# Decoder trunk on one core: the end by token halves, the sample's stores on ScalarE's queue, and the order of work at the borders

## The chip, the cores and the metric

One core of a Trainium2 chip runs the whole kernel. The metric is the device time of one execution in microseconds (us). The time before is the median of three runs; a further execution was profiled. The engines are PE (matmuls), DVE (VectorE), ACT (ScalarE), POOL (GpSimd) and SP (SyncE, which here issues the loads of weights and the stores).

## The reference

One decoder layer for 256 prompt tokens and 8 x 4 sample tokens, width 2048, all in fp32:

```
x = x + 1/2 * post1(SwiGLU_1(pre1(x)))
x = x + post2(HybridMixer(pre2(x)))
x = x + 1/2 * post3(SwiGLU_2(pre3(x)))
```

Each pre and post is an RMS norm over the 2048 columns with a gain. SwiGLU takes x to twice 5632 columns and back. The mixer projects x to q, k, v, a rank-16 product for the decay (a_lr), a gate r and the HGRN parts; it runs two gated linear recurrences (GLA and HGRN2) in chunks, norms, gates and projects back. The outputs are x of the prompt and of the sample tokens, and the final states.

## The kernel before

**Layout and matmuls.** Activations stay transposed: x[k], k = 0 to 15, is a tile of 128 columns of the model by T = 288 tokens (256 of the prompt, 32 of the samples). Weights come in units of 128 x 1024 fp32. ACT copies a unit to a high part wh (L96), and DVE subtracts it from the raw one to give the low part wl (L97), both in PE's fast fp32r format. Activations are split in the same way (xh, xl). A product is three matmuls: xh by wh, xl by wh, xh by wl (L591 to L593), with 288 tokens moving. The class Weights keeps up to four split units ahead of PE (HL_BUFS, three raw buffers); its field `behind` holds an instruction behind which the next split is ordered on DVE and ACT. A function block computes four 128-column outputs over all k, in PSUM tiles drawn from five banks, and evicts each.

**What sets the order.** A scheduler orders the instructions of each engine's queue, from the program's dependencies and its own estimates of time. `tc.issue_after(ins)` adds an order for what is traced inside it: behind ins on ins's engine, with no semaphore. Each engine serves its own queue strictly in order.

**Borders.** Ahead of a sub-layer, PreNorm (L473 to L505) sums the squares of x beside the first products: tick1(k) is called behind step k of a block, and at step `at` it calls rstd (L455 to L471). That issues the two `pre` matmuls (L460), then for FFNs a square root on ACT and a reciprocal (L463) on DVE of 128 x 288 to give the factor rt; in the mixer (`tmps` given) it goes by a logarithm, an exponential and two DVE steps (L470, L471). The products are not scaled until then, and their eviction multiplies by rt. Behind a sub-layer, post_norm (L558 to L575) sums the squares of its output y, spreads the factors over all partitions through PE (L445), and updates x: y by the factor (L562), x plus y by the gain (L563), then the split into xh on ACT (L257) and xl on DVE (L258). The first EARLY = 4 x tiles are covered by a stand-in: PE multiplies the old x and y (`fill`) with the first weights for one of the four outputs. UPDATED = 8 tiles are updated in this function.

**Mixer's start.** The first block (qk0) fills q and k of GLA's first heads; the second (v0) computes v, with a tick at each of its 16 steps k: at 11 the mean's matmuls, at 8 the scaling of the low-rank weights, at 12 a_lr, which multiplies x by the 16 columns (L1445, 16 products of 16 rows, 32 matmul instructions), adds four partial sums on DVE (L1449), scales them by rt (L1450) and splits them into high and low (L1451 to L1457). v's eviction multiplies by rt (L979). gla_decay multiplies them up later (zp, L1463). The next block that takes the banks is qk1.

**The end.** The last block of the last FFN writes y12 to y15. Its evictor ev (L750 to L775) adds a PSUM tile to y (L755), squares y (sq_add; for y15 on DVE at L422) and scales it by the gain to z (L764, ACT). by_token turns z to token-major with two PE transposes (L730) and an ACT copy (L731) into zT; samples does so for the 32 sample tokens (L737, L738) into zS. finish (L795 to L822) sums the squares per token with matmuls against ones (L432), takes root (ACT, L160) and reciprocal (DVE, L437) of two columns for the prompt's two halves of 128 tokens, then, behind POOL copies (L803), of one for the samples. Nine additions of 128 x 512 on DVE (L809) give the outputs: three pairs of the prompt, the samples, then the fourth pair. SP stores each prompt piece as it is ready (L822, 256 KB), and the samples in four stores (L815, 64 KB) between the third pair's and the fourth's.

Of the kernel before, what the change touches and what calls it, by code (L numbers as in the profile page):

```python
# [16 lines left out]
P = 128  # L17
# [109 lines left out]
def trunk_kernel(ctx, tc, x_prompt, x_sample, state_gla, state_hgrn, norm_gains, f1_in, f1_out, f2_in, f2_out,  # L127
# [37 lines left out]
    def mmtile(name):  # L165
        return mmp.tile([P, 512], F32, name=name, tag="mm")

    def auxtile(name):
        return aux.tile([P, 512], F32, name=name, tag="aux")
# [303 lines left out]
    class PreNorm:  # L473
# [12 lines left out]
        def tick1(self, k):  # L486
            if k < 8:
                with tc.issue_after(self.split[0]), tc.issue_after(self.split[1]):
                    for j in (2 * k, 2 * k + 1):
                        sq_add(x[j], j)  # L490
                    if k == 7:
                        self.parts = high_low(acc)
            if k == self.at:
                ins = rstd(rt, self.parts, self.name, self.tmps and self.tmps())

                behind = [G.memset(gate[:, 0:1], 0.0).ins, V.tensor_copy(gate[:, 1:2], epst).ins,
                          S.activation(gate[:, 2:3], epst, AF.Copy).ins]
                self.behind = behind
                with ExitStack() as es:
                    for i in behind:  # L500
                        order(i, ins)
                        es.enter_context(tc.issue_after(i))
                    for f in self.late:
                        f()
# [47 lines left out]
    def post_norm(gcol, gnext, lasts, name, fill):  # L552

        parts = [[sq[:, c:c + P] for c in (0, P, T - P)] for sq in (acc, *(sq for sq, _ in lasts))]
        rc, inss = mean_cols(auxtile(name), parts, 0, 3, True)
        fill.old_mean, fill.mean = inss[0], inss[-1]
        if name != "postm":
            with tc.issue_after(lasts[-1][1]):  # L558
                W.ahead(1)

        def update(k):
            V.tensor_tensor(y[k], y[k], fill.scale[:, 0:T], op=ALU.mult)  # L562
            ins = V.scalar_tensor_tensor(x[k], y[k], gcol(k), x[k], op0=ALU.mult, op1=ALU.add).ins  # L563
            return *split_x(gnext, k), ins

        def go():
            fill.scale, fill.row = spread(rc, name + "s")
            for k in range(UPDATED):
                with ExitStack() as es:
                    if k == 1:  # L570
                        es.enter_context(tc.issue_after(ins[2]))
                    ins = update(k)
                if k == AHEAD:
                    W.behind = ins[0]

        fill.go = go
        return update
# [64 lines left out]
    def ffn(tag, gcol, gnext, pn, before, fill=None):  # L642
# [3 lines left out]
        with ExitStack() as pools:  # L646
# [93 lines left out]
            def do_out(c, n):  # L740
                hs = [hid.pop(c + i) for i in range(n)]
                if final:
                    zt, xt = final_tiles[0:2]
                end = c + n == NCH
                if end:
                    act_set(AF.Sqrt)
                    if not final:
                        border[0].fill.old()
                for o in range(4):
                    def ev(f, ps):  # L750
                        k = 4 * o + f
                        if c == 0:
                            S.activation(y[k], ps, AF.Copy)
                        else:
                            V.tensor_tensor(y[k], ps, y[k], op=ALU.add)  # L755
                        if end:
                            sq = sq_add(y[k], k, 0, KT - 2, KT - 1)
                            if k >= KT - 1:
                                lasts.append(sq)
                            if not final:  # L760
                                border[0].fill.new(k)
                            else:
                                z = fp.tile([P, T], F32, name="z", tag="z", bufs=4)
                                S.activation(z, y[k], AF.Copy, scale=gcol(k))  # L764
                                if o < 3:
                                    turn32(z, f)
                                    if f == 3:
                                        move32(o, *zt, (G, nc.sync) if o == 2 else (G,))
                                else:
                                    if f > 1:  # L770
                                        by_token(zs[f - 2], k - 2, *zt)
                                    zs.append(z)
                    block(f"out{tag}_{c}_{o}", 4 * n, lambda k: [t[:, k % 4, :] for t in hs[k // 4]], ev,
                          tail=2 if end and o == 3 else 1, hold=end and o == 3)
                    k = 4 * (c - 4) + o  # L775
                    if final and 0 <= k < KT:
                        turn32(x[k], o)
                        if o == 3:
                            move32(c - 4, *xt, (G,))
# [3 lines left out]
            if final:  # L783
                zt, xt = final_tiles[0:2]

                def rest():
                    by_token(zs[2], KT - 2, *zt)
                    by_token(zs[3], KT - 1, *zt)
                    samples(zs, zt[1])

                finish(lasts[0][0], rest, zt, xt)
                return None
        return post_norm(gcol, gnext, lasts, f"post{tag}", border[0].fill), border[0]

    def finish(last, rest, zt, xt):  # L795

        (zT, zS), (xT, xS) = zt, xt
        ms = auxtile("postf")
        rc, _ = mean_cols(ms, [[sq[:, t * P:(t + 1) * P] for t in range(2)] for sq in (acc, last)], 0, 2, True)
        four = []  # L800
        for sq in (acc, last):
            r = sqp.tile([P, 4, TS], F32, name="sq4", tag="pn")
            G.tensor_copy(r, sq[:, TP:T].unsqueeze(1).broadcast_to([P, 4, TS]))  # L803
            four.append([r.rearrange("p a b -> p (a b)")])
        rest()
        rcs, _ = mean_cols(ms, four, 2, 3, False)

        def add(o, z, x, t):
            V.scalar_tensor_tensor(o, z, rc[:, t:t + 1] if t < 2 else rcs, x, op0=ALU.mult, op1=ALU.add)  # L809

        for s in range(4):
            if s == 3:
                add(zS, zS, xS, 2)
                for q in range(4):
                    nc.sync.dma_start(y_sample[:, :, q * 512:(q + 1) * 512].rearrange("b t c -> (b t) c"),  # L815
                                      zS[q * TS:(q + 1) * TS, :])

            o = (hlp if s else rawp).tile([P, 2, 512], F32, name=f"o{s}", tag="wh" if s else "raw")
            for t in range(2):
                k = slice(4 * s, 4 * s + 4)  # L820
                add(o[:, t].rearrange("p (k c) -> p k c", c=P), zT[:, k, t], xT[:, k, t], t)
                nc.sync.dma_start(y_prompt[0, t * P:(t + 1) * P, s * 512:(s + 1) * 512], o[:, t])  # L822


    def mixer(pn, border):
        with ExitStack() as mx:
# [614 lines left out]
            def a_lr():  # L1441
                ps = mmtile("a_lr")
                for k in range(KT):
                    q = k % 4 * TS
                    PE.matmul(ps[q:q + 16, 0:T], ag[:, k, :], x[k], start=k < 4, stop=k >= KT - 4)  # L1445
                G.memset(alr32[0:32, :], 0.0)
                S.activation(alr32[0:16, :], ps[0:16, 0:T], AF.Copy)
                for q in range(TS, P, TS):
                    V.tensor_tensor(alr32[0:16, :], alr32[0:16, :], ps[q:q + 16, 0:T], op=ALU.add)  # L1449
                V.tensor_tensor(alr32[0:16, :], alr32[0:16, :], rt[0:16, :], op=ALU.mult)  # L1450
                S.activation(alr[0:32, :], alr32[0:32, :], AF.Copy)  # L1451
                V.tensor_tensor(alr[32:64, :], alr32[0:32, :], alr[0:32, :].bitcast(F32), op=ALU.subtract)
                S.activation(alr[64:96, :], alr32[0:32, :], AF.Copy)
                for g in range(2):
                    c = slice(256 * g, 256 * g + 256)
                    S.activation(aw[:, c], aw32[g][0:96, 0:256], AF.Copy)
                    V.tensor_tensor(aw[64:96, c], aw32[g][64:96, 0:256], aw[64:96, c].bitcast(F32), op=ALU.subtract)  # L1457
# [30 lines left out]
            for g in range(2):  # L1488
# [5 lines left out]
                if g == 0:  # L1494
                    vt = vtiles("g0")
                    block("v0", KT, xrhs, ev_v(*vt, 2, 1), 
                          tick=lambda k: (pn.tick1(k), scale_lr() if k == 8 else a_lr() if k == 12 else None))
                    with tc.issue_after(W.recent[0]), tc.issue_after(W.recent[1]):
                        lower_bounds()

# [143 lines left out]
```

## Time and profile before

| | us |
|---|---|
| median of three runs (2248.39 to 2248.95) | 2248.5 |
| the profiled execution | 2247.12 |
| its span | 2245.3 |
| PE busy in the span | 2233.0 (99%) |
| DVE busy | 1386.3 (62%) |
| ACT busy | 1022.8 (46%) |
| POOL busy | 171.2 (8%) |

The mean granted clock of TensorE was 0.998. The DMA engines moved 171 GB/s in the mean. In a timeline a line gives the start, the length, the engine (SPq and ACTq: DMAs that SP or ACT issues), the line of the kernel, the operation, the tile written <- the tiles read, their shapes, and how many alike were merged; in brackets stands how long the engine had been idle and whom it waited for. The length of merged rows runs from the first one's start to the last one's end.

### The profile page before, as it was taken

To read this page: it belongs to the slowest core of one execution; us is meant where nothing else is said; L and a number is where in the kernel's file an instruction comes from. 1 tells how busy PE (TensorE), PEld (TensorE's weight loads), DVE (VectorE), ACT (ScalarE), POOL (GpSimd) and SP (SyncE) were. 2 spreads that over 40 slices of the span, in tenths; PEclk is the share of its full clock that TensorE was granted. 3 is DMA by queue.
4 is the path that set the end of the run, shared out by engine and by line. 5 is a ranking of instruction groups with operands and counts; after the bars stand their busy time and mean duration, and the time that the engine had idled before them with its cause. 6 is when DMAs were issued, how large, how long until landed. Compare 5 with 4: busy or idle time off the path is not lost.

```text
span 2245.3 us, 43325 instructions
## 1 busy us (share of the span) xinstructions
PE 2233.0 (99%) x17832; PEld 2218.3 (99%) x17832; DVE 1386.3 (62%) x2252; ACT 1022.8 (46%) x1556; POOL 171.2 (8%) x311
## 2 busy tenths in 40 slices
PE   9999999999999999999999999999999999999998
PEld 9999999999999999999999999999999999999998
DVE  7545545554555568888888755944555465545646
ACT  6443333333334345555676654544333333333344
POOL 2000000000000001333000000530000000000005
PEclk9999999999999999999999999999999999999999
DMA  7555555555555554667565554665555555555555
GB/s 223 171 169 162 167 168 162 168 167 163 169 165 182 170 164 141 194 197 213 174 172 169 178 184 130 195 186 164 165 169 164 165 169 164 165 169 163 166 166 152
DMA packets 226758, 384.28 MB, mean 171 GB/s; under 512 B 21106, under 2 KB 60544, under 8 KB 226560
## 3 DMA queue, kind: packets, MB, share of 16 engines
q1 hardware_dynamic: 213968, 365.15, 51.8%
q0 software_dynamic: 10416, 16.18, 2.7%
q8 instruction: 140, 2.29, 0.4%
q10 hardware_dynamic: 2176, 0.18, 0.1%
q14 instruction: 58, 0.48, 0.1%
HBM read 363.75 MB, written 11.80 MB: 167 GB/s over the span
## 4 chain that ended last, share of the span: by engine, by line
PE 99%; DVE 0%; POOL 0%; ACT 0%; issue 0%; DVEq 0%; POOLq 0%
PE gate L591 10%; PE gate L593 10%; PE gate L592 10%; PE out L592 8%; PE up L593 8%; PE up L591 8%; PE up L592 8%; PE out L593 8%; PE out L591 8%; PE hfq L591 2%; PE hfq L593 2%; PE hfq L592 2%; PE mo L593 2%; PE mo L591 2%; PE mo L592 2%; PE hi L591 1%
## 5 line engine op out<-in xcount | busy, mean ns | idle before, releaser
L97 DVE TENSOR_TENSOR wl<-raw,wh 128x1024 fp32r<-128x1024 f32 (+1 forms) x676 | 821.8, 1217 | 616.7 <-ACT wh L96 612.8
L96 ACT ACTIVATE wh<-raw 128x1024 fp32r<-128x1024 f32 (+1 forms) x676 | 711.5, 1054 | 1018.8 <-PE gate L592 308.8
L591 PE MATMUL gate<-xh,wh 128*128 128x288 f32 x1660 | 489.4, 296 | 0.0
L593 PE MATMUL gate<-xh,wl 128*128 128x288 f32 x1660 | 487.7, 295 | 0.0
L592 PE MATMUL gate<-xl,wh 128*128 128x288 f32 x1660 | 485.7, 295 | 0.0
L592 PE MATMUL out<-hl,wh 128*128 128x288 f32 x1408 | 416.1, 296 | 0.0
L593 PE MATMUL up<-xh,wl 128*128 128x288 f32 x1408 | 415.6, 295 | 0.0
L593 PE MATMUL out<-hh,wl 128*128 128x288 f32 x1408 | 415.3, 295 | 0.0
L592 PE MATMUL up<-xl,wh 128*128 128x288 f32 x1408 | 415.1, 295 | 0.0
L591 PE MATMUL up<-xh,wh 128*128 128x288 f32 x1408 | 415.0, 295 | 0.0
L591 PE MATMUL out<-hh,wh 128*128 128x288 f32 x1408 | 414.1, 294 | 0.0
L591 PEld LDWEIGHTS gate<-xh,wh 128*128 128x128 f32 x1660 | 311.3, 188 | 0.9 <-DVE z L1533 0.2
L593 PEld LDWEIGHTS gate<-xh,wl 128*128 128x128 f32 x1660 | 311.4, 188 | 0.2 <-DVE wl L97 0.2
L592 PEld LDWEIGHTS gate<-xl,wh 128*128 128x128 f32 x1660 | 310.7, 188 | 0.3
L593 PEld LDWEIGHTS out<-hh,wl 128*128 128x128 f32 x1408 | 265.0, 188 | 0.0
L591 PEld LDWEIGHTS out<-hh,wh 128*128 128x128 f32 x1408 | 264.9, 188 | 0.0
L592 PEld LDWEIGHTS out<-hl,wh 128*128 128x128 f32 x1408 | 264.7, 188 | 0.0
L593 PEld LDWEIGHTS up<-xh,wl 128*128 128x128 f32 x1408 | 264.6, 188 | 0.0
L592 PEld LDWEIGHTS up<-xl,wh 128*128 128x128 f32 x1408 | 264.4, 188 | 0.0
L591 PEld LDWEIGHTS up<-xh,wh 128*128 128x128 f32 x1408 | 264.3, 188 | 0.0
L755 DVE TENSOR_TENSOR y<-out,y 128x288 f32<-128x288 f32 x288 | 121.3, 453 | 101.3 <-PE out L593 98.3
L720 POOL DMA_DIRECT2D zT<-b x40 | 23.2, 586 | 721.7 <-issue 721.7
(396 smaller groups left out, 2573.2 us busy)
## 6 DMA issues: line engine op xcount, KB each, us to landing
raw<-in_ffn_w_in_dram SPq DMA_DIRECT2D x350, 512.0 KB, 3.5
raw<-in_ffn_w_out_dram SPq DMA_DIRECT2D x176, 512.0 KB, 3.6
raw<-in_mix_w_in_dram SPq DMA_DIRECT2D x64, 512.0 KB, 4.0
raw<-in_mix_w_in_dram SPq DMA_DIRECT2D x96, 256.0 KB, 3.2
raw<-in_mix_w_out_dram SPq DMA_DIRECT2D x32, 512.0 KB, 3.7
out_dram<-s POOLq DMA_DIRECT2D x32, 256.0 KB, 2.8
s<-in_state_gla_dram SPq DMA_DIRECT2D x16, 256.0 KB, 4.7
s<-in_state_hgrn_dram SPq DMA_DIRECT2D x16, 256.0 KB, 5.3
```

Of the source, the lines that this page charges most:

```text
L96: i1 = self.nc.scalar.activation(h[:, c], raw[:, c], AF.Copy).ins
L97: i2 = self.nc.vector.tensor_tensor(l[:, c], raw[:, c], h[:, c].bitcast(F32), op=ALU.subtract).ins
L591: yield lambda: PE.matmul(dst, w[0][:, c:c + P], parts[0], start=start, stop=False)
L592: yield lambda: PE.matmul(dst, w[0][:, c:c + P], parts[1], start=False, stop=False)
L593: yield lambda: PE.matmul(dst, w[1][:, c:c + P], parts[0], start=False, stop=stop)
L720: queues[n % len(queues)].dma_start(dst[q * TS:(q + 1) * TS, 4 * g:4 * g + 4, :, cols].rearrange("p k t c -> p (k t) c"), b32[rows, q])
L755: V.tensor_tensor(y[k], ps, y[k], op=ALU.add)
```

## The change

1. **Borders, weight split.** In PreNorm.tick1, where `tmps` is not given (before both FFNs), the next weight split is ordered behind the reciprocal: on DVE wl comes behind it and, in the order that the scheduler gives, also behind the gate copy and up to four of the first products' scalings by rt (L658).
2. **Borders, x tiles in order.** In post_norm's go(), tiles 1, 2 and 3 are each ordered behind the update before, where only tile 1 was. DVE's order of y by the factor (y), update (x) and low part (xl) goes from y0 x0 y1 y2 xl0 x1 x2 y3 xl1 xl2 x3 to y0 x0 y1 x1 xl0 y2 xl1 x2 y3 y4 xl2 x3.
3. **Low-rank products two steps up.** a_lr's matmuls, its copy and the adds go to step 10 of v0, and the rest (now lr_parts) stays at step 12. On PE the 32 instructions now lie ahead of step 11 and of the two `pre` matmuls. The scheduler also moves the neighbours: qk1_0 takes eight matmuls first where it took three; the zp products come fifteen matmuls later; on DVE the scaling of the low-rank sums, one weight split, two mask steps and alr lie ahead of v_0's eviction.
4. **The end.** y15 is evicted and squared in two parts, of 128 and 160 tokens; each of the prompt's halves has a PSUM tile, a root and a reciprocal of its own (128 x 1); z15 moves behind the samples' root on ACT, and the transposes of z13 to z15 behind the last sum on PE. DVE's order becomes: reciprocal 0, o0 first half, reciprocal 1, o1 first half, o0 and o1 second half, reciprocal 2, o2 both, samples, o3 both. The sample's four stores are issued by ACT; SP has only the eight of the prompt.

PE has the same number of instructions in both kernels; DVE has three more.

```diff
@@ PreNorm.tick1
                 ins = rstd(rt, self.parts, self.name, self.tmps and self.tmps())
+                if self.tmps is None:
+                    W.behind = ins
@@ post_norm, go()
-                    if k == 1:
+                    if 1 <= k < EARLY:
                         es.enter_context(tc.issue_after(ins[2]))
@@ ev of the last block
+                        elif final and end and k == KT - 1:
+                            sq = sqp.tile([P, T], F32, name="sq", tag="sq")
+                            with ExitStack() as es:
+                                for r in (slice(0, P), slice(P, T)):
+                                    V.tensor_tensor(y[k][:, r], ps[:, r], y[k][:, r], op=ALU.add)
+                                    ins = V.tensor_tensor(sq[:, r], y[k][:, r], y[k][:, r], op=ALU.mult).ins
+                                    es.enter_context(tc.issue_after(ins))
+                            lasts.append((sq, None))
...
-                            else:
+                            elif k < KT - 1:
@@ rest
-                def rest():
-                    by_token(zs[2], KT - 2, *zt)
+                def rest(ins, tot):
+                    with tc.issue_after(tot):
+                        for i in (1, 2):
+                            by_token(zs[i], KT - 4 + i, *zt)
+                    z = fp.tile([P, T], F32, name="z", tag="z", bufs=4)
+                    with tc.issue_after(ins):
+                        S.activation(z, y[KT - 1], AF.Copy, scale=gcol(KT - 1))
+                    zs.append(z)
                     by_token(zs[3], KT - 1, *zt)
                     samples(zs, zt[1])
@@ finish
+        mss = [mmtile(f"postf{t}") for t in range(2)]
+        rc = [colp.tile([P, 1], F32, name=f"rc{t}", tag=f"rc{t}", bufs=1) for t in range(3)]
...
+        def scale(t):
+            ins = act(rc[t], mss[t % 2][:, t:t + 1], AF.Sqrt, bias=epst)
+            V.reciprocal(rc[t], rc[t])
+            return ins
+
+        for sq in (acc, last):
+            for t in range(2):
+                total(sq[:, t * P:(t + 1) * P], t, sq is acc, sq is last)
+        scale(0)
+        scale(1)
...
+        for i in range(2):
+            tot = total(four[i], 2, False, i == 1)
+        behind = scale(2)
+        rest(behind, tot)
...
+        for t in range(2):
+            for s in range(3):
+                prompt(s, t)
+        add(zS, zS, xS, 2)
+        for q in range(4):
+            S.dma_start(y_sample[:, :, q * 512:(q + 1) * 512].rearrange("b t c -> (b t) c"), zS[q * TS:(q + 1) * TS, :])
+        for t in range(2):
+            prompt(3, t)
@@ a_lr, v0
+
+            def lr_parts():
                 V.tensor_tensor(alr32[0:16, :], alr32[0:16, :], rt[0:16, :], op=ALU.mult)
...
-                          tick=lambda k: (pn.tick1(k), scale_lr() if k == 8 else a_lr() if k == 12 else None))
+                          tick=lambda k: (pn.tick1(k), scale_lr() if k == 8 else a_lr() if k == 10 else lr_parts() if k == 12 else None))
```

More of the change, by code (lines that the diff above doesn't have):

```diff
@@ L753, in ev @@
                             S.activation(y[k], ps, AF.Copy)
+                        elif final and end and k == KT - 1:
[6 more added lines that the diff above has]
+                            lasts.append((sq, None))
                         else:
                             V.tensor_tensor(y[k], ps, y[k], op=ALU.add)
-                        if end:
+                        if end and not (final and k == KT - 1):
                             sq = sq_add(y[k], k, 0, KT - 2, KT - 1)
@@ L759, in ev @@
                                 lasts.append(sq)
+                        if end:
                             if not final:
                                 border[0].fill.new(k)
-                            else:
+                            elif k < KT - 1:
                                 z = fp.tile([P, T], F32, name="z", tag="z", bufs=4)
@@ L797, in finish, with total @@
         (zT, zS), (xT, xS) = zt, xt
-        ms = auxtile("postf")
-        rc, _ = mean_cols(ms, [[sq[:, t * P:(t + 1) * P] for t in range(2)] for sq in (acc, last)], 0, 2, True)
+        mss = [mmtile(f"postf{t}") for t in range(2)]
+        rc = [colp.tile([P, 1], F32, name=f"rc{t}", tag=f"rc{t}", bufs=1) for t in range(3)]
+        def total(cols, t, start, stop):
+            return PE.matmul(mss[t % 2][:, t:t + 1], cols, onesD[:, 0:1], start=start, stop=stop, skip_group_check=True).ins
+        def scale(t):
[7 more added lines that the diff above has]
+        scale(1)
         four = []
@@ L803, in finish, with prompt @@
             G.tensor_copy(r, sq[:, TP:T].unsqueeze(1).broadcast_to([P, 4, TS]))
-            four.append([r.rearrange("p a b -> p (a b)")])
-        rest()
-        rcs, _ = mean_cols(ms, four, 2, 3, False)
-        def add(o, z, x, t):
[L809 to L822, printed above, removed]
+            four.append(r.rearrange("p a b -> p (a b)"))
+        for i in range(2):
+            tot = total(four[i], 2, False, i == 1)
+        behind = scale(2)
+        rest(behind, tot)
+        def add(o, z, x, t):
+            V.scalar_tensor_tensor(o, z, rc[t], x, op0=ALU.mult, op1=ALU.add)
+        outs = [(hlp if s else rawp).tile([P, 2, 512], F32, name=f"o{s}", tag="wh" if s else "raw") for s in range(4)]
+        def prompt(s, t):
+            k, o = slice(4 * s, 4 * s + 4), outs[s][:, t]
+            add(o.rearrange("p (k c) -> p k c", c=P), zT[:, k, t], xT[:, k, t], t)
+            nc.sync.dma_start(y_prompt[0, t * P:(t + 1) * P, s * 512:(s + 1) * 512], o)
+        for t in range(2):
[6 more added lines that the diff above has]
+            prompt(3, t)
     def mixer(pn, border):
```

## Prediction

> **What bounds the kernel now.** I read the page first, then the waits of the matmul engine, then the timelines of the places that the diff touches, and last the end of the span by slices.
>
> ```profile
> span 2245.3 us, 43325 instructions
> PE 2233.0 (99%) x17832; PEld 2218.3 (99%) x17832; DVE 1386.3 (62%) x2252; ACT 1022.8 (46%) x1556; POOL 171.2 (8%) x311
> ...
> PE warm L306 <- POOL onesD L229: 1.1, 1, 1.1
> PE postf L432 <- DVE sq L422: 0.2, 1, 0.2
> PE qk L591 <- DVE y L979: 0.2, 1, 0.2
> PE zp L1463 <- POOL qm L902: 0.2, 1, 0.2
> ```
>
> PE is busy for 2233.0 of 2245.3 us. The four rows with L306 to L1463 are all that the view of waits lists for it (us in total, times, longest). Two, qk and zp, lie in the mixer at the step that the change moves, one (postf) at the end. So no edit in the body can give more than a fraction of a microsecond unless it takes matmuls away, and this one takes none: both instruction lists have the same number on PE. What is left is the end, where PE has no more weight products:
>
> ```profile
> 2231.97 0.46 DVE L755 TENSOR_TENSOR y<-out,y 128x288 f32<-128x288 f32 x1 [0.36 <-PE out L593]
> 2232.46 0.46 DVE L422 TENSOR_TENSOR sq<-y 128x288 f32<-128x288 f32 x1
> 2233.91 0.17 DVE L437 RECIPROCAL rc<-rc 128x2 f32<-128x2 f32 x1 [0.99 <-ACT rc L160]
> 2234.11 2.74 DVE L809 SCALAR_TENSOR_TENSOR o<-zT,rc,xT 128x512 f32<-128x512 f32 x4
> 2236.77 0.16 DVE L437 RECIPROCAL rc<-rc 128x1 f32<-128x1 f32 x1
> 2236.84 1.40 DVE L809 SCALAR_TENSOR_TENSOR o<-zT,rc,xT 128x512 f32<-128x512 f32 x2
> 2238.15 0.75 DVE L809 SCALAR_TENSOR_TENSOR zS<-zS,rc,xS 128x512 f32<-128x512 f32 x1
> 2238.81 1.41 DVE L809 SCALAR_TENSOR_TENSOR o<-zT,rc,xT 128x512 f32<-128x512 f32 x2
> ...
> 2234.89 3.70 SPq L822 DMA_DIRECT2D out_dram<-o  x6
> 2238.93 2.12 SPq L815 DMA_DIRECT2D out_dram<-zS  x4
> 2241.14 0.88 SPq L822 DMA_DIRECT2D out_dram<-o  x2
> ...
> DMA to landing us min/median/max: 2.2/2.3/2.4
> ...
> DMA to landing us min/median/max: 1.6/1.8/1.9
> ...
> 2236.00:2237.00 1.00, 0.00 (x0) 0.00 (x0) 1.00 (x4) 0.00 (x0) 0.00 (x0) 1.00 1.04 383
> 2240.00:2241.00 1.00, 0.00 (x0) 0.00 (x0) 0.22 (x1) 0.00 (x0) 0.00 (x0) 0.50 0.44 113
> ```
>
> First DVE, then SP's DMA issues (start, length), then the landing times of L822 (prompt stores, 256 KB each) and of L815 (sample stores, 64 KB each), then two slices (their last two columns are the DMA share and GB/s). DVE is through with its last addition at 2238.81 + 1.41 = 2240.22, but the last store is issued near 2241.6 (the last two take from 2241.14 to 2242.02), because four sample stores stand ahead of it in SP's queue and take 2.12 us to issue. At 2.4 us to landing it is down at 2244.0, and the span ends 1.3 us later. The slices say the same: the DMA engines are full (1.04, 383 GB/s) while DVE feeds them, then drop to 0.44 and 113 GB/s while SP issues the samples. That hole is what the end can give back. The profiled execution took 2247.12, 1.8 over its span, and is 1.4 under the median of the three timed runs (2248.5).
>
> **The end, part by part.** Today the sum of squares starts when the square of y15 is whole, 2232.92; PE sums, ACT takes the root, DVE the reciprocal:
>
> ```profile
> 2232.97 0.61 PE L432 MATMUL postf<-onesD,sq 128*128 128x1 f32 x4 [0.21 <-DVE sq L422]
> ...
> 2233.08 0.53 ACT L764 ACTIVATE z<-y,hg 128x288 f32<-128x288 f32 x1
> 2233.62 0.26 ACT L160 ACTIVATE rc<-postf,epst 128x2 f32<-128x2 f32 x1
> ...
> L1109 DVE TENSOR_TENSOR F<-F 128x144 f32<-128x144 f32 x1 | 0.3, 306 | 0.0
> ```
>
> In halves, DVE does add and square of 128 columns, then of 160. No row here has these sizes from PSUM; 144 columns take 306 ns and 288 take 0.46 us, so I take 0.29 and 0.32. The first square is ready at 2231.97 + 0.29 + 0.03 + 0.29 = 2232.58, 0.34 sooner; the second at 2233.2, 0.25 later. The sum of the first half needs two of the four matmuls, 0.38 instead of 0.61, so its root starts at 2233.05 and not 2233.62 (z15, 0.53 on ACT, no longer lies ahead of it; it would have ended at 2233.61). Root 0.26, reciprocal 0.17 and two handovers of 0.03 give a first addition at **2233.54 for 2234.11, -0.57**. If a half costs as much as a whole (0.46), the first square is ready at 2232.92 as before, the second 0.95 later, and only the matmuls' 0.23 and the 0.04 of ACT are won; that is the other bound. The second half's root follows about 2233.65, and its reciprocal stands behind the first addition on DVE, which covers it. The z15 that moves behind the third root, and the transposes of z13 to z15 behind PE's last sum, feed only the fourth pair of additions and the samples. ACT then has three roots, z15, three zT copies and zS in a row, done near 2236.7; the samples' addition wants zS at about 2237.7. Margin 1 us, so nothing.
>
> DVE keeps nine additions and has one reciprocal more (0.07 of spacing, from 2236.77 to 2236.84), so its last addition ends at 2240.22 - 0.57 + 0.07 = 2239.72.
>
> The trade of queues counts for more. SP has only its eight stores, so the last is issued as its addition ends, 2239.75 instead of 2241.6; at 2.35 to landing that is **2242.1 instead of 2244.0**. The four sample stores go out on ACT, which has nothing else left, from about 2238.4. ACT's price for an issue of its own is in this row:
>
> ```profile
> 60.41 0.40 ACTq L865 DMA_DIRECT2D araw<-in_mix_w_in_dram  x1
> ```
>
> At SP's spacing (2.12 / 4 = 0.53) the last goes out at 2240.0 and lands, with 1.9, at 2241.9, about with the prompt's. Now the bytes: eight stores of 256 KB and four of 64 KB are 2.36 MB, at 380 GB/s 6.2 us. The first bytes now move some 0.8 us after the first issue, near 2235.1, so the engines alone cannot be done before 2241.3, and DVE's pace sets the end, by a little. I take **-1.8 us**. Bounds: -2.5, where the landing is by bytes alone, to -0.5, where only the start is won and the sample stores land last.
>
> The Trainium skill speaks against this part: DMA: Bandwidth & Descriptors, section "Issuing engines are not separate DMA queues", says that DMAs of all issuing engines run on the same 16 engines, and that a second issuer saves only the sequencer's time, usually small beside the DMA. By that rule the queue's trade would be worth near nothing; the trace has it otherwise at this place, with engines at 0.44 while SP issues.
>
> **The mixer.** The low-rank products go ahead of the mean's matmuls.
>
> ```profile
> 901.10 2.13 PE L1445 MATMUL a_lr<-x,y 128*16 128x288 f32 x32
> ...
> 902.21 0.46 DVE L471 SCALAR_TENSOR_TENSOR rt<-rsls,rslsg 128x288 f32<-128x288 f32 x1
> 903.75 0.82 DVE L1436 SCALAR_TENSOR_TENSOR k_g<-k_g,rt 128x288 f32<-128x288 f32 x2
> 907.07 1.21 DVE L97 TENSOR_TENSOR wl<-raw,wh 128x1024 fp32r<-128x1024 f32 x1
> 908.21 0.44 DVE L1450 TENSOR_TENSOR y<-y,rt 16x288 f32<-16x288 f32 x1
> 908.68 1.19 DVE L979 TENSOR_TENSOR y<-v,rt 128x288 f32<-128x288 f32 x3
> 911.09 0.45 DVE L1452 TENSOR_TENSOR alr<-y,alr 32x288 fp32r<-32x288 f32 x1
> ...
> 904.91 1.06 ACT L96 ACTIVATE wh<-raw 128x1024 fp32r<-128x1024 f32 x1 [0.67 <-PE v L592]
> ...
> 909.19 0.40 PE L591 MATMUL qk<-xh,wh 128*128 128x288 f32 x1 [0.18 <-DVE y L979]
> ```
>
> The 32 matmul instructions take 2.1 us, so rt, now ready at 902.67, comes at 904.8. On DVE then stand the gate, the selectors and the q and k scalings (from rt's end to 904.57 now, 1.9 us), y by rt (0.4), a split wl (1.2), two small mask steps (0.3, estimated from the 0.3 of the 144-column row) and alr (0.45), and only then the eviction of v_0: 904.8 + 1.9 + 0.4 + 1.2 + 0.3 + 0.4 + 0.4 = 909.4. PE wanted qk's next bank 0.2 to 0.3 before 909.19; in the new order it takes two matmuls of qk1_0 more first, at 0.13 each, and wants v_0's bank near 909.1. So a gap of 0.3 stays there, for the 0.2 of the waits view. The other gap, zp's 0.2, should close: zp comes fifteen matmuls (2.0 us) later in PE's order, while y by rt, from which its operands come, ends near 907.1 and not at 908.65; against that a wh copy (1.06) now lies ahead of the last operand on ACT. Sum **-0.2**; bounds -0.5 (both gaps gone) and +2.2 (a weight split's pair ahead of v_0, below).
>
> **The borders.**
>
> ```profile
> 856.36 0.56 PE L592 MATMUL qk<-xl,wh 128*128 128x288 f32 x3
> 857.02 0.40 PE L591 MATMUL qk<-xh,wh 128*128 128x288 f32 x1
> ...
> 856.43 0.97 ACT L257 ACTIVATE xh<-x,prm 128x288 fp32r<-128x288 f32 x2 [0.27 <-DVE x L563]
> ```
>
> After the first FFN, PE's one gap lies before 857.02, where x1's high part comes from ACT. Matmuls of 0.30 that take 0.56 in three start 0.13 apart, so the next would have started at 856.76: 0.26 lost. In order, x1 comes two DVE steps (y2 and xl0, 0.4 each) earlier, which closes it; x3 stands behind one step more (y4) and is then late by about 0.4. I take **+0.1**, bounds -0.3 and +0.4. The other border has no gap, and x3 comes just in time there: 0, bounds 0 and +0.4.
>
> The split of the two other borders goes behind the reciprocal.
>
> ```profile
> 56.83 1.95 DVE L463 RECIPROCAL rt<-rt 128x288 f32<-128x288 f32 x1
> ...
> 58.81 1.56 DVE L658 TENSOR_TENSOR g<-g,rt 128x288 f32<-128x288 f32 x4
> ```
>
> The unit's low part comes behind both rows, 3.7 us later (1.95, 0.15 of gate and copy, 1.56), and rt 0.8 sooner. Splits are held up to four units ahead, and a unit is 24 matmuls, 3.2 us at 0.13: the delay is a little over one unit of four, no wait of PE for wl is in the view of waits, and nothing on PE waits for rt. So I put 0; up to +1 where the lead is short.
>
> **Sum:** -1.8 - 0.2 + 0.1 = -1.9, so about 2245.2 for the profiled execution's 2247.12, and on the median's footing 2248.5 - 1.9 = **2246.6**.
>
> **Rivals.**
> (a) *The stores set the end.* Sample and prompt stores meet on full engines, and the 64 KB ones, of 32 rows, land last. For: 1.04 at 383 GB/s while DVE feeds. Against: the hole of 0.44 right behind. Then the early start and a little more are left, -0.7 in all: 2247.8. The rule of the page above would come out here.
> (b) *v_0's eviction comes late: slower than before.* DVE serves in order; if the split ahead of v_0 waits for its wh copy on ACT (some 2.3 us for copy and subtraction), PE stands at qk1_1 behind a wait which the change itself adds. It decides from an eviction at about 911.3, 1.9 behind the 909.4 above: then the forecast gain is eaten. With 2.2 lost and x3 late at both borders (0.4 each), 2248.5 - 1.8 + 2.2 + 0.8 = 2249.7. For: rt is 2.1 later, and no slack is left. Against: ACT copies that wh at 904.91 as its buffer comes free, 1 us ahead of its turn on DVE.
> (c) *The body's edits do nothing*: the border order only moves the wait from x1 to x3 and the mixer's gaps change place, and the end alone counts: 2246.7, inside the likeliest case.
>
> **How the numbers follow.** Likeliest, with (c): 0.66, 2245.8 to 2247.3. Rival (a) 0.17, rival (b) 0.11; 0.06 for something that no row shows, either way. The range is the likeliest case with the lower bounds of the end, the mixer and the border (-2.5, -0.5, -0.3) below, and (a) and part of (b) above: 2245.2 to 2249.2. A measurement of this kernel can tell about 0.2%, 4.5 us: faster means under 2244.0, slower over 2253.0. No case above reaches either, so only the unseen 0.06 does, in part: faster 0.03, slower 0.04, same 0.93.
>
> **What would show it.** At the end: y15's two additions and two squares at 0.3 each, an output addition 0.6 sooner behind PE's last weight product (1.6 us for 2.2), four sample stores on ACT's queue at 0.4 to 0.5 each, DMA slices that stay near 1 until the last landing, and that landing 2.4 us behind DVE's last addition instead of 3.8. In the mixer: PE's waits ahead of qk1_1 and zp. At the borders: a gap before x3's products. I am wrong if PE gains over 1 us in the body, if the samples land more than 0.5 us behind the last prompt store, or if v_0's eviction ends after 911.

## The result and the profile after

| | before | after |
|---|---|---|
| median of 13 runs each, us | 2248.73 (2248.24 to 2249.12) | 2253.42 (2252.59 to 2255.97) |
| ratio, 95% interval | | 1.0023 (1.0016 to 1.0031) |
| profiled execution, us | 2247.12 | 2255.48 |
| its span | 2245.3 | 2253.7 |

The change makes the kernel 4.7 us **slower**, where 1.9 us faster was forecast. The profiled execution of after is one of its longer ones, 2.1 us over the median, and that of before one of its shorter ones, 1.6 under; the spans of the two differ by 8.4, so sizes are read from parts of them and not from the whole.

Head of the page of after, then PE's view of waits (us in total, times, longest):

```profile
span 2253.7 us, 43326 instructions
...
PE 2241.8 (99%) x17832; PEld 2225.4 (99%) x17832; DVE 1385.8 (61%) x2255; ACT 1023.3 (45%) x1557; POOL 169.5 (8%) x311
```

```profile
PE warm L306 <- POOL onesD L229: 1.1, 1, 1.1
PE sc L1203 <- DVE k_h L1143: 0.6, 1, 0.6
PE postf L819 <- DVE sq L761: 0.6, 2, 0.4
PE qk L593 <- DVE y L1015: 0.3, 1, 0.3
PE gate L593 <- DVE u L676: 0.2, 1, 0.2
PE out L593 <- DVE y L765: 0.2, 1, 0.2
PE gate L593 <- DVE z L1571: 0.2, 1, 0.2
```

PE has the same 17832 instructions and is busy for 8.8 us more, while its waits have grown by 1.5 us in all; the mean granted clock is 0.998 in both. So PE does not wait for anything new that is large: its work itself takes longer. Of the 8.8, 1.2 lies behind the last weight product (4.16 us busy there for 2.96): the same sums and transposes run there, but in after the granted clock is 0.51 from 2243.0 to 2245.5, while in before it is 1.00 until 2236. The view by windows shows where most of the rest lies. These rows cover the whole run but only the instructions of one tile; behind the window's length stands PE's busy time with its count, then PEld's. First out (the FFNs' second product) and up (a part of the first) in before, then in after:

```profile
0.00:2250.00 2250.00, 562.65 (x4224) 560.31 (x4224) 121.26 (x288) 12.73 (x32) 1.00 0.55 171
...
0.00:2250.00 2250.00, 564.40 (x4224) 561.55 (x4224) 38.02 (x88) 1.00 0.55 171
```

```profile
0.00:2250.00 2250.00, 568.60 (x4224) 565.86 (x4224) 121.28 (x289) 12.88 (x32) 1.00 0.58 171
...
0.00:2250.00 2250.00, 564.39 (x4224) 561.54 (x4224) 37.81 (x88) 1.00 0.58 171
```

Out takes 568.60 for 562.65, 5.95 us more for the same 4224 matmuls (1.4 ns each), and up nothing more. In the timelines the starts of the gate blocks fall behind before's by 0.29 to 0.30 us at nearly every chunk of 512 hidden columns, and all of it in the out block. The diff does not touch that block's instructions (but for the eviction of y15, on DVE). What it does touch is where their operands lie. finish takes three small tiles rc0 to rc2 of its own in the pool `colp`; each takes 32 bytes of every partition, and this pool lies below the FFN's and the mixer's. In the compiled programs hh and hl (the FFN's hidden values in a high and a low part, which out multiplies) stand at bytes 145664 and 154880 of the partition before and at 145760 and 154976 after, **96 bytes higher**; x, xh, xl, wh, wl stand where they were. That is where the loss lies; that the shift causes it is shown by e1, e2 and e5 below. Some 3 us of the 8.4 lie neither in out nor at the end: a start 0.5 later, waits here and there. Another profile of the same instructions (e5 below, span 2245.7) has 1.2 of them, and one with the end's edits alone (e6) has 2.1, in part at other places. So they vary from one execution to the next, and what share of them the edits have stays open.

The end did what was forecast on the engines and less in the queues. First the timeline of after's end (DVE, SP, ACT), then the landing times of the prompt's stores and of the sample's (minimum, median, maximum), then slices, with the DMA share and GB/s last:

```profile
2241.05 0.29 DVE L760 TENSOR_TENSOR y<-out,y 128x128 f32<-128x128 f32 x1 [0.38 <-PE out L595]
...
2242.63 0.75 DVE L842 SCALAR_TENSOR_TENSOR o<-zT,rc,xT 128x512 f32<-128x512 f32 x1
...
2247.43 1.41 DVE L842 SCALAR_TENSOR_TENSOR o<-zT,rc,xT 128x512 f32<-128x512 f32 x2
...
2243.41 5.79 SPq L849 DMA_DIRECT2D out_dram<-o  x8
...
2247.55 1.92 ACTq L856 DMA_DIRECT2D out_dram<-zS  x4
```

```profile
DMA to landing us min/median/max: 2.1/2.2/3.0
```

```profile
DMA to landing us min/median/max: 1.8/2.5/2.9
```

```profile
2248.00:2249.00 1.00, 0.00 (x0) 0.00 (x0) 0.84 (x2) 0.00 (x0) 0.00 (x0) 0.50 0.83 268
2249.00:2250.00 1.00, 0.00 (x0) 0.00 (x0) 0.00 (x0) 0.00 (x0) 0.00 (x0) 0.50 0.90 219
2250.00:2251.00 1.00, 0.00 (x0) 0.00 (x0) 0.00 (x0) 0.00 (x0) 0.00 (x0) 0.50 1.04 375
```

On a clock that starts with PE's last weight product (2231.63 in before, 2240.71 in after), the first addition starts at 1.92 instead of 2.48, DVE is done at 8.13 instead of 8.59, and the last prompt store is issued at 8.16 instead of 9.97. But it takes 3.0 to land instead of 2.4, and is down at 11.16 instead of 12.35. The last sample store, issued at 8.36, takes 2.9 and is down at 11.29. In two of the slices the DMA engines are busy at 0.83 and 0.90 and move 268 and 219 GB/s. The span ends 1.7 behind the last sample store, here and in e5 and e6; in before it ended 1.3 behind the last prompt store. So it ends 12.99 behind that product instead of 13.67: 0.7 won.

### The profile page after: what moved, and what is told of

Same layout as the page of the kernel before. It is cut to its first block, busy times and chain, and to the rows that moved or that the text cites. A ratio compares the mean times of both kernels' runs of the same rounds, so it can differ in the third digit from the quotient of the medians.

```text
span 2253.7 us, 43326 instructions
## 1 busy us (share of the span) xinstructions
PE 2241.8 (99%) x17832; PEld 2225.4 (99%) x17832; DVE 1385.8 (61%) x2255; ACT 1023.3 (45%) x1557; POOL 169.5 (8%) x311
```

## The experiments

Each runs beside the kernel before on the same chip; the medians of before were 2248.07 (e1 to e4), 2248.35 (e5 to e8), 2248.21 (e9 to e12) and 2248.17 (e13 to e15). An interval of a ratio is here some 0.9 thousandths to either side, 2 us (1.3 in e11 and e15, which have five runs each).

**e1 to e4: is it the addresses?** Theory A: hh and hl lost an alignment. Rival B: the edited instructions are slower. Rival C: what counts is the distance from hh to other tiles.

```diff
     colp = ctx.enter_context(tc.tile_pool(name="colp", bufs=2))
+    pads = [colp.tile([P, 1], F32, name=f"pad{t}", tag=f"pad{t}", bufs=1) for t in range(3)]
```

That is e1, on before; e2 has one such tile on after, e3 two on before. e4 on before:

```diff
+    pad0 = xpool.tile([P, 24], F32, name="pad0")
     xh = [xpool.tile([P, T], F32R, name=f"xh{k}") for k in range(KT)]
     xl = [xpool.tile([P, T], F32R, name=f"xl{k}") for k in range(KT)]
+    pad1 = xpool.tile([P, 8], F32, name="pad1")
```

> Before, with three idle 4-byte tiles in the pool of the small columns, and nothing else: each takes 32 bytes, so every tile behind that pool (hh, hl, the mixer's q, k, v) stands 96 bytes higher, as in the changed kernel. Theory A (the 96 bytes alone make PE's down-projection matmuls slower, because hh and hl lose their alignment): the out products go from 132.4 to 133.7 ns apart, 22 times 0.30 us per chunk, so 5.5 to 7 us more than before, 2254 to 2255.5. Rival B (the changed instructions slow the kernel: the mixer's late eviction, the borders, the queues): as before within 0.5 us, 2248.7.

Measured: 2254.0, ratio 1.0025 (1.0015 to 1.0034). Idle tiles of 96 bytes alone make the kernel before as slow as after.

> After, with one more idle 4-byte tile in the same pool: 128 bytes instead of 96, so hh is again at a multiple of 128 bytes. All instructions are those of after. Theory A: the out products are back at 132.4 ns, and what the edits do by themselves is left: 2247 to 2249. Rival B: 2253.4, as after. Rival C (not the alignment but the distance of hh from other tiles): also 2253 or any other time, since the distance to xh and wh has changed again.

Measured: 2248.25, ratio 1.0001 (0.9992 to 1.0010). With 32 bytes more, after is as fast as before.

> Before, with two idle tiles: hh 64 bytes higher, at 64 over a multiple of 128, as xh, wh and wl are placed anyway. Theory A with a step of 64 bytes: within 1 us of before (2248.7), out products at 132.4 to 132.6 ns. Theory A with a step of 128 bytes: near 2254, as e1. Rival C: any time.

Measured: 2250.2, ratio 1.0009 (1.0001 to 1.0018): 2.1 slower, between the two.

> Before, with 96 idle bytes ahead of xh and 32 behind xl: xh and xl are 96 bytes higher, at 32 over a multiple of 64, and all tiles behind them 128 higher, hh so at a multiple of 128. Theory A: now the products that read xh and xl (gate, up and the mixer's, about 11,000 of the 17,000) slow down by the 1.3 ns that hh's did, while out stays: 12 to 16 us over before, 2261 to 2265. Rival B and a cause peculiar to hh: 2248.7.

Measured: 2248.95, ratio 1.0001 (0.9993 to 1.0010). Theory A's 12 to 16 us did not come. Out in e1 and e2, out and up in e4:

```profile
0.00:2250.00 2250.00, 568.18 (x4224) 565.76 (x4224) 121.24 (x288) 12.77 (x32) 1.00 0.55 171
```

```profile
0.00:2250.00 2250.00, 563.31 (x4224) 561.01 (x4224) 121.39 (x289) 12.83 (x32) 1.00 0.55 171
```

```profile
0.00:2250.00 2250.00, 562.70 (x4224) 560.20 (x4224) 121.22 (x288) 12.74 (x32) 1.00 0.54 171
...
0.00:2250.00 2250.00, 564.73 (x4224) 561.87 (x4224) 38.04 (x88) 1.00 0.54 171
```

Rival B falls with e1 and e2 (568.18 with no edit, 563.31 with all). Theory A falls with e4: xh and xl lie off every multiple of 64 and up takes 564.73 for 564.40. But in e4 the three kinds of product did change, against each other: the times from start to start of xh by wh went from 132.2 to 133.2 ns, of xl by wh from 132.6 to 132.1, of xh by wl from 133.0 to 132.7 (means over up's matmuls in the trace). So addresses matter, but not as the alignment of one tile alone.

**A fourth theory.** With each matmul's addresses from the program, the start-to-start times of before, e1, e3 and e4 sort by the distance from the weights to the moving tile, modulo 512 bytes (the residue): 131.65 ns at 64, 131.4 to 131.7 at 256, but 133.2 at 192, 133.4 at 128 and 135.3 at 32. Between before and e4, which moves hh and the weights together by 128, the four values of out agree within 0.03. A tile is 1152 bytes long, 128 over a multiple of 512, so neighbours take four residues each: hh had 64, 192, 320, 448 (132.4 in the mean), and after has 32, 160, 288, 416 (133.7). Theory D: this distance decides.

Single executions speak for it too. In the first FFN's last three chunks 240 of out's products take their weights from another buffer (from byte 212960 on), so that the same hh and hl lie at other residues from them: 32, 160, 288 and 416 in before, 0, 128, 256 and 384 in after. In before these took 133.45 ns, and their neighbours in the same chunks 132.35; in after it is the other way round, 132.72 and 133.43.

**e5 to e8: the edits by themselves,** at before's addresses. e5 on after:

```diff
-        rc = [colp.tile([P, 1], F32, name=f"rc{t}", tag=f"rc{t}", bufs=1) for t in range(3)]
+        rcs = colp.tile([P, 3], F32, name="rc", tag="rc")
+        rc = [rcs[:, t:t + 1] for t in range(3)]
```

e6 is e5 without the edits to the mixer and the borders; e7 is before with `a_lr() if k == 10 else lr_parts() if k == 12` alone; e8 is before with `W.behind = ins` and `1 <= k < EARLY` alone.

> After, with its three reciprocals in the columns of one tile, as before had them: every large tile stands at the very address that it had in before, every instruction and its order are those of after. If the 96 bytes were all of the loss, the out products are back at 132.4 ns and the rest is what the edits do: the end gives 0.7 (last weight product to the end of the span took 13.67 in before and 12.99 in after), mixer and borders lose up to 1, so 2247.5 to 2248.7 where before is at 2248.1. By the prediction's own terms (end -1.8, mixer -0.2, borders +0.1) it would be 2246.2.

Measured: 2247.76, 0.6 under before; ratio 0.9998 (0.9989 to 1.0006).

> Before with the end's edits alone, at before's addresses. As after's end was seen: 0.7 faster, 2247.4 for 2248.1, last store down 11.3 us behind the start of PE's last weight product instead of 12.4. By the prediction: 1.8 faster. If the end gave nothing: 2248.1.

Measured: 2247.46, 0.9 under; ratio 0.9998 (0.9989 to 1.0006).

> Before with the low-rank products two steps up alone. By the prediction 0.2 faster; by its rival (v_0's eviction late) 2.2 slower; by the trace of after, whose starts of blocks fall 1.4 us behind between v and the output projection with part of that not from the addresses, 0.3 to 1 slower: 2248.4 to 2249.1 where before is at 2248.1.

Measured: 2248.17, 0.2 under; ratio 1.0000 (0.9991 to 1.0008).

> Before with the two border edits alone (split behind the reciprocal, x tiles in order). By the prediction 0.1 slower, within 0.5 either way of 2248.1. If the weight split's delay opens gaps before both FFNs, as the trace of after shows one of 0.4 us near 1450, up to 0.8 slower.

Measured: 2249.16, 0.8 over; ratio 1.0004 (0.9995 to 1.0013).

All four hold no change within their intervals, so the sizes of the parts rest on the traces, and the medians can't confirm them. Out took 562.66 us in e5, as in before:

```profile
0.00:2250.00 2250.00, 562.66 (x4224) 560.31 (x4224) 121.31 (x289) 12.86 (x32) 1.00 0.55 171
```

The mixer's place in e5:

```profile
909.63 0.29 PE L594 MATMUL qk<-xl,wh 128*128 128x288 f32 x1
910.26 0.40 PE L593 MATMUL qk<-xh,wh 128*128 128x288 f32 x1 [0.34 <-DVE y L1016]
...
914.49 0.29 PE L593 MATMUL qk<-xh,wh 128*128 128x288 f32 x1
914.79 0.51 PE L1502 MATMUL zp<-alr,ahl 96*128 96x288 f32 x2
```

From start to start with the usual 0.13 taken off, PE loses 0.50 ahead of qk1_1 (0.34 in before) and 0.17 ahead of zp (0.32). The sum of the two is the same; only a third gap, ahead of the first scores (`sc`), shrank from 0.19 to 0.09.

**e9 to e11: theory D against theory A.** e9 is before with `pad0 = xpool.tile([P, 8], F32)` behind acc and the three idle tiles of e1; e10 is e5 with `pad1 = xpool.tile([P, 16], F32)` behind xl; e11 is e10 with

```diff
-    xh = [xpool.tile([P, T], F32R, name=f"xh{k}") for k in range(KT)]
-    xl = [xpool.tile([P, T], F32R, name=f"xl{k}") for k in range(KT)]
+    xh = [xpool.tile([P, 320], F32R, name=f"xh{k}")[:, 0:T] for k in range(KT)]
+    xl = [xpool.tile([P, 320], F32R, name=f"xl{k}")[:, 0:T] for k in range(KT)]
```

> Before, with 32 idle bytes behind x's tiles and 96 behind the small columns: the weights (raw, wh, wl) stand 32 bytes higher, hh and hl 128, xh and xl where they were. The traces so far, sorted by the distance of the moving tile from its weights modulo 512 bytes, give the mean start-to-start time of four neighbouring tiles (1152 bytes apart, so at four residues 128 apart): residues 64, 192, 320, 448: 132.3 ns; 0, 128, 256, 384: 132.7; 96, 224, 352, 480: 132.7; 32, 160, 288, 416: 133.8. Theory D (the distance decides): hh goes from the 64s to the 32s, so out products at 133.7 ns as in after, and 5 to 7 us more than before, though hh is at a multiple of 128; xh goes from the 0s to the 96s, no change. Theory A (hh's own alignment): no change, within 1 us.

Measured: 2252.73, ratio 1.0020 (1.0011 to 1.0029): 4.5 slower, with hh at a multiple of 128. The sign is D's, the size a little under it: 133.3 ns in the mean, since the residue 32 took 133.1 here and not 135.3.

> After at before's addresses, with 64 idle bytes behind xl: weights, hh and hl stand 64 bytes higher, xh and xl where they were. Theory D: hh keeps its distance (the 64s) and its 132.4 ns; xh and xl go from the 0s to the 64s, from 132.6 to 132.3 ns on 11,880 products: 2.7 to 4.4 us less than the same kernel without it, 2243.4 to 2245.1 where before is at 2248.3. Theory A: hh is at 64 over a multiple of 128, as in before with 64, and the time is 1 to 2 us longer instead: 2249 to 2250.

Measured: 2247.19, ratio 0.9996 (0.9987 to 1.0005): 1.0 under before, where e5 was 0.6 under. Out kept its time, as D has it, and A's loss did not come. But up did not gain: the residue 448 took 133.0 ns here where out had 132.2, and the mean stayed at 132.6.

> As the weights 64 higher, and the tiles of xh and xl 1280 bytes apart instead of 1152, so that their distances take only two residues, 64 and 320. Theory D: by the same table 131.65 and 132.2 ns, so 0.7 ns less on 11,880 products: 7 to 9 us less than after at before's addresses, 2239 to 2241 where before is at 2248.3. If only the residue modulo 128 counted, it would be as with the weights 64 higher.

Measured: **2238.95, ratio 0.9962 (0.9948 to 0.9975)**: 9.3 faster than before, and the first of these kernels that is faster by more than its interval. Out in e9, up in e11:

```profile
0.00:2250.00 2250.00, 566.39 (x4224) 563.96 (x4224) 121.21 (x288) 12.74 (x32) 1.00 0.54 171
```

```profile
0.00:2250.00 2250.00, 560.71 (x4224) 557.81 (x4224) 37.96 (x88) 1.00 0.54 171
```

Up is at 560.71 for 564.40, 0.87 ns less for each matmul, in a block where only the places of xh, xl and the weights changed.

**e12 to e15: which part costs what.** e12 is before with `W.behind = ins` alone, e14 with `1 <= k < EARLY` alone; e13 is e6 with `nc.sync.dma_start` for the sample's stores; e15 is before with the tiles of e11.

> Before with the first border edit alone: the weight split behind the reciprocal before both FFNs, the x tiles as before. The two border edits together measured 0.8 slower. If the split's delay is the cause: 2249.1 where before is at 2248.3. If it is the order of the x tiles: 2248.3. By the prediction, which puts this edit at 0: 2248.3.

Measured: 2247.92, ratio 0.9999 (0.9990 to 1.0007).

> The end's edits alone, with the sample's four stores on SP as before. The prediction gave 0.5 of the end to the earlier and 0.07 later additions and 1.3 to the change of queue; the end alone measured 0.9 and its trace shows the last store 1.8 us sooner issued but only 0.7 to 1.2 sooner down. If the queue's trade is worth the rest (0.3 to 0.5): 2247.7 to 2248.0 where before is at 2248.3. If it is worth 1.3 as the prediction put it: no gain or a loss, 2248.3 to 2248.8.

Measured: 2248.25, ratio 0.9999 (0.9990 to 1.0008).

```profile
2234.81 3.82 SPq L848 DMA_DIRECT2D out_dram<-o  x6
2238.95 2.16 SPq L855 DMA_DIRECT2D out_dram<-zS  x4
2241.21 0.87 SPq L848 DMA_DIRECT2D out_dram<-o  x2
```

PE's last weight product starts at 2232.12 there, and the last prompt store is down 11.95 later, between before (12.35) and e6 (11.32). In e6 the last sample store comes behind it, at 11.36, and the end of the span 1.7 behind that. By the span's end, 13.7 in before, 13.3 in e13 and 13.1 in e6, the earlier additions alone bring 0.4 of their 0.56, and the queue adds 0.2 to that, where 1.3 was reckoned.

> Before with the order of the x tiles alone. By the difference of both border edits (0.8 slower) and the split alone (0.3 faster, within the noise): 0.3 to 1 slower, and two gaps of about 0.25 on PE after the first FFN instead of one. By the prediction's sum: 0.1 slower.

Measured: 2249.34, 1.2 over before; ratio 1.0004 (0.9995 to 1.0013). ACT, DVE and PE at the border after the first FFN:

```profile
856.97 0.41 ACT L545 ACTIVATE fsum<-fill 128x288 f32<-128x288 f32 x1 [0.37 <-PE fill L593]
857.28 0.53 ACT L257 ACTIVATE xh<-x,prm 128x288 fp32r<-128x288 f32 x1
...
857.84 0.52 DVE L258 SCALAR_TENSOR_TENSOR xl<-x,prm,xh 128x288 fp32r<-128x288 f32 x1
858.27 0.52 DVE L563 SCALAR_TENSOR_TENSOR x<-y,hg,x 128x288 f32<-128x288 f32 x1
...
858.76 0.56 PE L592 MATMUL qk<-xl,wh 128*128 128x288 f32 x3
859.41 0.41 PE L591 MATMUL qk<-xh,wh 128*128 128x288 f32 x1
...
860.33 0.56 PE L592 MATMUL qk<-xl,wh 128*128 128x288 f32 x3
861.00 0.40 PE L591 MATMUL qk<-xh,wh 128*128 128x288 f32 x1
```

The gap at x1 is gone, and two stand in its place, at x2 and x3, 0.25 and 0.27 over the usual 0.13. xl1 now lies ahead of x2 on DVE and waits for xh1, which waits on ACT behind the copy of the stand-in's sum. That is 0.25 net. By the starts of the blocks, from the last out block ahead of this border to the mixer's gate block, e14 falls 0.3 behind before and e12 not at all. The rest of the 1.2 in the median is within the interval; this profile's other delays lie elsewhere, 1.1 us of them ahead of the border, and their cause stays open.

> Before, no edit of the change, with xh and xl 1280 bytes apart and 64 idle bytes behind them. Theory D (the distance between the moving tile and its weights modulo 512 decides, whatever the instructions do): the same 8 to 9 us as on the changed kernel, 2239 to 2240.5. If a part of that gain came from the change's edits: less.

Measured: 2239.79, ratio 0.9961 (0.9948 to 0.9973), 8.4 faster. Up in e15:

```profile
0.00:2250.00 2250.00, 560.70 (x4224) 557.84 (x4224) 38.00 (x88) 1.00 0.58 171
```

The gain needs none of the edits.

## Why the prediction was wrong, point by point

**The step that failed** stands in the first part: "So no edit in the body can give more than a fraction of a microsecond unless it takes matmuls away, and this one takes none". It reads a change as a change of instructions and takes the time of a matmul as fixed. The sum had a term for each edit and none for the tiles that the edits allocate; three tiles of 4 bytes cost 5.95 us in the out blocks (e1: 5.9 by the medians). No rival had this either: rival (b), the slower side, looked for a wait. What came is in the 0.06 for something that no row shows. Its place could have been seen without a run, since the pool lies ahead of hh in the program's memory. Its price could in part have been read too: before's own trace has the 240 products at the residues that after gave to all the others, 1.1 ns slower than their neighbours, and 1.1 ns on 4224 matmuls is an estimate of 4.6 us.

**The end** had the right mechanism and the wrong size: -1.8 forecast, -0.7 by the trace and -0.9 by the median of e6 (whose interval holds no change). First addition -0.57 forecast and -0.56 measured, DVE's end -0.5 and -0.46, last prompt store's issue -1.85 and -1.81. The terms that failed come behind it: the landing, 2.35 forecast and 3.0 measured for the last prompt store; the last sample store, forecast ahead of it, landed 0.13 behind; and from the last landing to the end of the span it took 1.7 and not 1.3. Sample and prompt stores meet at that point and the samples land last, as rival (a) said, whose -0.7 is what came. The sentence of the Trainium skill (DMA: Bandwidth & Descriptors, "Issuing engines are not separate DMA queues") was nearer than my reading of it: the last prompt store's issue came 1.8 sooner and the span ended 0.7 sooner, and of that the queue's trade brought 0.2 (e13 against e6). The slice of 0.44 that I held against it showed free engines, but not how fast they would move small and large stores together (219 to 268 GB/s).

**The mixer** came near the forecast of -0.2 by luck: -0.1 in the gaps of e5, and that from a third gap that the prediction did not name; e7's median, -0.2, has an interval of 2 us to either side. The terms written, +0.1 at v_0's eviction and -0.2 at zp, also add up to -0.1 and not to -0.2. In the view of waits the first is as forecast (0.3 for 0.2), but from start to start it grew from 0.34 to 0.50, and zp's did not close (0.17 left). Rival (b)'s 1.9 did not come.

**The borders:** the split behind the reciprocal costs nothing that can be seen (in e12 PE waits where it did in before, and as long), as forecast. The order of the x tiles was put at +0.1; PE's gaps say +0.25, since not x3 alone but x2 too comes late. I had left out that xl1 waits for ACT, which has the sum's copy ahead.

**Together** the edits are worth what e5 shows, 0.6 faster with an interval that holds zero, and with the 96 bytes the change is 4.7 slower.

## What to carry to other kernels

Before the instructions of a change are priced, compare where both programs put the tiles that the busiest engine reads: here a small tile in an early pool moved all that lies behind it. Where an engine is busy for 99%, group its busy time by block and divide by the count; one per cent more in one block, on unchanged instructions, pointed here to the operands' places. Effects of edits as small as these can only be compared with all large tiles at the same addresses, and a pitch chosen for the tiles was worth more here than the edits.

## What the runs showed of the hardware that was not expected

The same matmul (128 x 128 weights, 288 columns of fp32r) took from 131.4 to 135.3 ns from start to start in the mean of a group, by the place of its moving tile relative to its weights. Over ten profiles the best means by residue modulo 512 were 131.5 at 256 and 131.75 at 64, the worst 134.5 at 32, with 133.2 to 133.5 at 128, 384 and 192. That rule sorts most of it and predicted e11, e15 and the sign of e9, but not all: the same residue differed by up to 2 ns between kernels (32: 135.3 in e1, 133.1 in e9), and e10's gain was missed. The period of 512 isn't settled either: residues 256 apart mostly agree (133.4 at 128 and 133.5 at 384), but not all do (133.2 at 192, 132.4 at 448). The next matmul counts as well: in before, out's products at 448 took 131.7 ns where the next one had the same residue and 133.3 where it had 320. What in the chip makes it so, and whether the work of other engines has a share, no run here tells.
